# Where a matmul's stream begins in SBUF relative to its weights: 448 instead of 32 bytes, modulo 512

## The chip, the cores and the metric

The kernel runs on one core of a Trainium2 chip. The metric is the device time of one execution in microseconds; a kernel is run several times and the median is taken. PE is the matmul engine (its weight loads are profiled apart, as PEld), DVE, ACT and POOL are the vector, scalar and general engines, and SP issues the transfers.

## What is computed

A decoder trunk of two layers on 256 tokens of width 1024, all in float32. The part that the change is about is the feed-forward block and the projections around it:

```python
for layer in range(DEPTH):
    h = rmsnorm(x, norm_mix[layer])
    z = h @ w_in[layer]
    ...
    x = x + jnp.concatenate([o_a, o_b, o_c, o_d], axis=-1) @ w_out[layer]
    h = rmsnorm(x, norm_ffn[layer])
    x = x + (jax.nn.silu(h @ w_gate[layer]) * (h @ w_up[layer])) @ w_down[layer]
return rmsnorm(x, norm_final)
```

The four head groups (o_a to o_d) are small attention and matrix-memory mixers on 64-wide heads. The hidden width of the feed-forward block is 2816.

## The kernel before, in words

Every weight matrix streams in once, in units of 128 rows by 1024 columns (512 KB). `weight_unit` (line 226) issues the transfer into `wraw`, lets ACT round it to `whi` and DVE form the rest, `wlo`; each of the three tiles has four buffers. Activations are kept in the same two halves, so a product is made of three matmuls: high times high, high times low, low times high.

A matmul has a stationary operand, 128x128, which PE loads first, and a moving operand, which it streams, up to 512 columns of four bytes in each partition. The kernel uses both assignments:

- **The activations are stationary, the weights stream.** `columns` (line 909) for the input projection (tile `zp`, 512 or 404 columns at a time), and `wide` (line 1048) for the second layer's w_down (tiles `dn`, 512 columns, and `dnl`, 256 columns).
- **The weights are stationary, the activations stream.** `wide_T` (line 955) for w_out (tile `op`, the stream is `oT`) and for the first layer's w_down (tile `dn`, the stream is `gT`), and `columns_T` (line 940) for gate and up of both layers (tile `f`, the stream is `hT`).

In the second case `product_T` (line 245) makes the product. Where an accumulator has a whole bank (512 columns), one matmul streams both halves of the activations, 512 columns, against `whi` (line 250), and a second one streams the high half, 256 columns, against `wlo` (line 251). This text calls the two a pair. Where an accumulator has half a bank, `product` (line 240) makes three matmuls of 256 columns (lines 241 to 243). Half banks: all of w_out, the first two of the eleven groups of 512 columns of each layer's gate and up, and two of the eight output blocks of the first layer's w_down. All the rest of gate, up and the first w_down goes in pairs.

`shifted` (line 271) sets where the activations begin inside their tile. If they will be streamed, it skips `SHIFT` elements (line 31), else none:

```python
def shifted(a, n, moving):
    a = a[:, SHIFT if moving else 0:]
    return a[:, 0:n * 2 * SEQ].rearrange("p (k a t) -> p k a t", a=2, k=n)
```

`Norm` uses it for `hT` (line 282; moving for the feed-forward block, not for the input projection), and line 1082 for `gT` (moving in the first layer only). All slices of `hT`, `gT`, `oT` and of the weights that are stationary begin at multiples of 512 bytes from the start of their region, so the distance between a stream's first byte and its weights' first byte, modulo 512, is the same for every matmul of a stage.

PE runs its instructions in the order written; the table `ORDER` interleaves the mixers with the input projection, and the feed-forward block has PE to itself.

Of the kernel before, what the change touches and what calls it, by code (L numbers as in the profile page):

```python
# [10 lines left out]
F32 = mybir.dt.float32  # L11
F32R = mybir.dt.float32r
BF = mybir.dt.bfloat16
AF = mybir.ActivationFunctionType
# [4 lines left out]
P = 128  # L19
# [8 lines left out]
DEPTH = 2  # L28
EPS = 1e-6
WARM = 11  # L30
SHIFT = 8
PAD = 8
MID0 = 2
TAIL = 2
# [70 lines left out]
def trunk(ctx, tc, xt, w_in, w_out, w_gu, w_dn, gains, gfin, cmpw, chan, rowp, ident_d, kf, kb, out):  # L105
    nc = tc.nc
    V, S, G, T = nc.vector, nc.scalar, nc.gpsimd, nc.tensor

    const = ctx.enter_context(tc.tile_pool(name="const", bufs=1))
    par = ctx.enter_context(tc.tile_pool(name="par", bufs=1))  # L110
    wp = ctx.enter_context(tc.tile_pool(name="wp", bufs=2))
    work = ctx.enter_context(tc.tile_pool(name="work", bufs=1))
# [24 lines left out]
    def kc(n, rows=P):  # L137
        return kft[0:rows, KOFF[n]:KOFF[n] + _KC[n]]
# [50 lines left out]
    def bcast(ap):  # L189
        return ap.partition_broadcast(P)  # L190

    def load_positions(l):
        d = {'ch': par.tile([P, 554], F32, name="chan")}
        nc.sync.dma_start(d['ch'][:, 0:32], chan[l, :, 0:32])
        d['posr'] = d['ch'][:, 0:32].rearrange("p (q m c) -> p q m c", q=8, m=2)
        return d

    def load_params(l, d):
        ch = d['ch']
        nc.sync.dma_start(ch[:, 32:], chan[l, :, 32:])  # L200
        d['conv'] = ch[:, 32:42].rearrange("p (b j) -> p b j", b=2)
        d['wqk'] = ch[:, 42:554].rearrange("p (i b n) -> p i b n", i=2, b=2)
        rw = par.tile([P, 456], F32, name="rowp")
        nc.sync.dma_start(rw, bcast(rowp[l]))
        d['gateb'] = rw[:, 0:8]
        d['mnorm'] = rw[:, 8:264]
        d['lamv'] = rw[:, 264:392].rearrange("p (a b) -> p a b", a=4)
        d['dnorm'] = rw[:, 392:456]

        lam_init = 0.8 - 0.6 * math.exp(-0.3 * l)  # L210
        lp = par.tile([P, 2, 32], F32, name="lp")
        ls = par.tile([P, 2], F32, name="ls")
        V.tensor_tensor(out=lp, in0=d['lamv'][:, 0:4:2, :], in1=d['lamv'][:, 1:4:2, :], op=OP.mult)
        V.tensor_reduce(out=ls, in_=lp, op=OP.add, axis=AX.X)
        le = par.tile([P, 2], F32, name="le")
        S.activation(le, ls, AF.Exp)
        d['nlam'] = par.tile([P, 1], F32, name="nlam")
        V.scalar_tensor_tensor(out=d['nlam'], in0=le[:, 1:2], scalar=-lam_init, in1=le[:, 0:1],
                               op0=OP.add, op1=OP.subtract)
        d['subg'] = par.tile([P, HD], F32, name="subg")  # L220
        V.tensor_scalar(d['subg'], d['dnorm'], 1.0 - lam_init, None, op0=OP.mult)
        d['hgh'] = par.tile([P, 256], F32, name="hgh")
        V.tensor_scalar(d['hgh'], d['mnorm'], 0.5, None, op0=OP.mult)
# [47 lines left out]
# [7 lines that stand above are left out]
    class Norm:  # L278
        def __init__(self, g, moving):
            self.g = g  # L280

            hl = shifted(work.tile([P, KB * 2 * SEQ + SHIFT], F32R, name="hT", bufs=1), KB, moving)
            self.x2 = [hl[:, k] for k in range(KB)]
# [79 lines left out]
    def mixer_a(l, z, d):  # L363
# [41 lines left out]
        for c in range(2):  # L405
# [3 lines left out]
                        in1=kc('bdk')[:, :, None].to_broadcast([P, 2, NCMP]), op=OP.mult)  # L409
# [3 lines left out]
                        in1=kc('bd60')[:, :, None].to_broadcast([P, NH, HD]), op=OP.mult)  # L413
# [13 lines left out]
                T.matmul(pcs[:, (t * 2 + b) * 30:(t * 2 + b + 1) * 30], q0[:, b, t * P:(t + 1) * P],  # L427
                         kcb.rearrange("p a n -> p (a n)"), start=True, stop=True)
        yield
        gs = par.tile([P, 2, 12], F32, name="gs")  # L430
        S.activation(gs, z[:, :, COL['ag']:COL['ag'] + 12], AF.Tanh, scale=0.5)
        V.tensor_scalar(gs, gs, 0.5, 0.5, op0=OP.mult, op1=OP.add)

# [418 lines left out]
    d = None  # L852
    for l in range(DEPTH):
# [18 lines left out]
        def group(f):  # L872
            o = work.tile([P, 2, 256], F32, name="o", bufs=2)
            yield from f(l, z, d, o)
            return o

        fs = dict(Z=lambda: mixer_a(l, z, d), A=lambda: mixer_a2(l, z, d), C=lambda: group(mixer_c),
                  B=lambda: group(mixer_b), D=lambda: group(mixer_d))
        gens = {}

        def emit(steps):
            for token in steps.split():
                n = token[0]
                if n == 'w':
                    cur['cmpw'] = [weight_unit(cmpw[l, :, u * 1024:(u + 1) * 1024]) for u in range(2)]
                    continue
                if n == 'p':
                    load_params(l, d)
                    load_consts()
                    continue  # L890
                if n in 'acbd':
                    finish('acbd'.index(n), cur[n.upper()])
                    continue
                if n not in gens:
                    gens[n] = fs[n]()
                for _ in range(int(token[1:] or 1)):
                    try:
                        next(gens[n])
                    except StopIteration as r:
                        cur[n] = r.value  # L900
                        if n == 'A':
                            oT[0] = r.value
# [173 lines left out]
        if l + 1 < DEPTH:  # L1076
            d = load_positions(l + 1)
            load_params(l + 1, d)
        else:
            gf = work.tile([P, D], F32, name="gfin", tag="hT", bufs=1)  # L1080
            nc.sync.dma_start(gf, bcast(gfin[0]))
        gT = shifted(bigp.tile([P, NFB * 2 * SEQ + SHIFT], F32R, name="gT", tag="big"), NFB, l + 1 < DEPTH)

# [227 lines left out]
```

## Time and profile before

| | |
|---|---|
| median of 3 runs | 666.11 us (664.45 to 667.17) |
| the profiled execution | 665.1 us |
| its span, first to last instruction | 663.3 us |
| granted PE clock, share of full speed | 0.994 |
| PE busy | 649.6 us of 3993 matmul records |
| DVE, ACT, POOL busy | 481.4, 384.4, 50.6 us |

The span is what the trace shows; the profiled execution's own time lies 1.8 us above it. A matmul's listed duration holds its passage through the array too, and matmuls overlap, so the step from the start of one to the start of the next is the time that it costs. The timeline gives these starts.

### The profile page before, as it was taken

The numbers are of one execution on the slowest core, as the hardware profiler recorded it, in microseconds if no ns is written. First come the engines' busy times: TensorE is split into PE (matmuls) and PEld (weight loads), VectorE is DVE, ScalarE is ACT, GpSimd is POOL, SyncE is SP. The second block draws the span as 40 slices with busy tenths as digits, with TensorE's granted clock in tenths as the row PEclk, the third lists the DMA queues.
The fourth block names the chain that finished last, engine by engine and source line by source line (L and its number), as shares of the span: only waits on it lengthen the run. The fifth ranks groups of instructions, "written<-read, shape, count | busy, mean of one in ns | idle before, by whom it ended". The sixth has DMA issues, their size and how long they took to land.

```text
span 663.3 us, 10576 instructions
## 1 busy us (share of the span) xinstructions
PE 649.6 (98%) x3993; PEld 566.1 (85%) x3993; DVE 481.4 (73%) x814; ACT 384.4 (58%) x692; POOL 50.6 (8%) x67
## 2 busy tenths in 40 slices
PE   9989999999999999999999999999999999999996
PEld 6877787899988888999988777889998888888885
DVE  6697887768777877744588978875867777875443
ACT  7555776545565656533376487664655656564332
POOL 0000031100200111000010001041000000000002
PEclk9999999999999999999999999999999999999998
DMA  8856305245566666666638441332566666667631
GB/s 269 268 184 201 114 5 171 69 139 173 172 208 188 188 184 197 190 191 190 182 125 275 148 127 33 103 121 83 152 212 171 192 185 195 190 189 221 188 122 63
DMA packets 32882, 109.09 MB, mean 164 GB/s; under 512 B 4032, under 2 KB 5696, under 8 KB 32832
## 3 DMA queue, kind: packets, MB, share of 16 engines
q1 hardware_dynamic: 32544, 107.91, 53.8%
q8 instruction: 31, 0.51, 0.3%
q10 hardware_dynamic: 288, 0.52, 0.2%
q14 instruction: 19, 0.16, 0.1%
HBM read 107.37 MB, written 1.05 MB: 163 GB/s over the span
## 4 chain that ended last, share of the span: by engine, by line
PE 91%; DVE 4%; ACT 2%; issue 1%; POOL 1%; POOLq 0%; ACTq 0%; DVEq 0%
PE f L250 20%; PE f L251 10%; PE zp L242 6%; PE zp L243 6%; PE zp L241 6%; PE dn L250 5%; PE dn L242 3%; PE dn L241 3%; PE dn L243 3%; PE dn L251 2%; PE f L241 2%; PE f L243 2%; PE f L242 2%; PE op L242 2%; PE op L243 2%; PE op L241 2%
## 5 line engine op out<-in xcount | busy, mean ns | idle before, releaser
L237 DVE TENSOR_TENSOR wlo<-wraw,whi 128x1024 fp32r<-128x1024 f32 (+2 forms) x204 | 242.9, 1192 | 111.9 <-ACT whi L236 110.9
L236 ACT ACTIVATE whi<-wraw 128x1024 fp32r<-128x1024 f32 (+2 forms) x204 | 210.8, 1035 | 173.7 <-PE f L250 45.9
L250 PE MATMUL f<-hT,whi 128*128 128x512 f32 x576 | 199.8, 390 | 0.0
L251 PE MATMUL f<-hT,wlo 128*128 128x256 f32 x576 | 162.4, 282 | 0.0
L250 PEld LDWEIGHTS f<-hT,whi 128*128 128x128 f32 x576 | 108.1, 188 | 22.6
L251 PEld LDWEIGHTS f<-hT,wlo 128*128 128x128 f32 x576 | 108.9, 189 | 0.0
L242 PE MATMUL zp<-wlo,hT 128*128 128x512 f32 (+1 forms) x192 | 76.1, 397 | 2.6 <-DVE wlo L237 2.6
L241 PE MATMUL zp<-whi,hT 128*128 128x512 f32 (+1 forms) x192 | 74.4, 398 | 0.9 <-ACT whi L236 0.9
L243 PE MATMUL zp<-whi,hT 128*128 128x512 f32 (+1 forms) x192 | 75.2, 392 | 0.0
L250 PE MATMUL dn<-gT,whi 128*128 128x512 f32 x132 | 46.7, 390 | 0.0
L242 PEld LDWEIGHTS zp<-wlo,hT 128*128 128x128 f32 x192 | 36.4, 190 | 9.5 <-DVE wlo L237 4.7
L241 PEld LDWEIGHTS zp<-whi,hT 128*128 128x128 f32 x192 | 36.4, 191 | 7.4 <-ACT whi L236 2.0
L243 PEld LDWEIGHTS zp<-whi,hT 128*128 128x128 f32 x192 | 36.3, 189 | 5.0
L251 PE MATMUL dn<-gT,wlo 128*128 128x256 f32 x132 | 37.2, 282 | 0.0
L241 PE MATMUL f<-hT,whi 128*128 128x256 f32 x128 | 36.5, 285 | 0.0
L243 PE MATMUL op<-oT,wlo 128*128 128x256 f32 x128 | 36.3, 284 | 0.0
L241 PE MATMUL op<-oT,whi 128*128 128x256 f32 x128 | 36.3, 284 | 0.0
L242 PE MATMUL op<-oT,whi 128*128 128x256 f32 x128 | 35.9, 280 | 0.0
L243 PE MATMUL f<-hT,wlo 128*128 128x256 f32 x128 | 35.7, 279 | 0.0
L242 PE MATMUL f<-hT,whi 128*128 128x256 f32 x128 | 35.7, 279 | 0.0
L250 PEld LDWEIGHTS dn<-gT,whi 128*128 128x128 f32 x132 | 24.8, 188 | 4.4
L242 PE MATMUL dn<-wlo,gT 128*128 128x512 f32 x66 | 26.0, 394 | 0.0
(299 smaller groups left out, 1157.9 us busy)
## 6 DMA issues: line engine op xcount, KB each, us to landing
wraw<-in_w_gu_dram SPq DMA_DIRECT2D x88, 512.0 KB, 3.9
wraw<-in_w_dn_dram SPq DMA_DIRECT2D x44, 512.0 KB, 3.7
wraw<-in_w_in_dram SPq DMA_DIRECT2D x36, 512.0 KB, 4.5
wraw<-in_w_out_dram SPq DMA_DIRECT2D x16, 512.0 KB, 3.5
wraw<-in_w_in_dram SPq DMA_DIRECT2D x8, 404.0 KB, 3.2
wraw<-in_w_in_dram SPq DMA_DIRECT2D x8, 256.0 KB, 4.4
wraw<-in_cmpw_dram SPq DMA_DIRECT2D x4, 512.0 KB, 4.8
xr<-in_xt_dram SPq DMA_DIRECT2D x8, 128.0 KB, 4.2
```

Of the source, the lines that this page charges most:

```text
L236: S.activation(hi[:, c], raw[:, c], AF.Copy)
L237: V.tensor_tensor(out=lo[:, c], in0=raw[:, c], in1=hi[:, c].bitcast(F32), op=OP.subtract)
L241: T.matmul(acc, xh, wh, start=first, stop=False)
L242: T.matmul(acc, xh, wl, start=False, stop=False)
L243: T.matmul(acc, xl, wh, start=False, stop=last)
L250: T.matmul(acc, wh, x2.rearrange("p a t -> p (a t)"), start=first, stop=False)
L251: T.matmul(acc[:, 0:SEQ], wl, xh, start=False, stop=last)
```

## The change

The constant `SHIFT` goes from 8 to 112 elements, 32 to 448 bytes. That makes the tiles of `hT` and `gT` 416 bytes longer in each partition. To make room and to set the places of what lies behind, the small tile `le` is dropped (the exponential is written over its input `ls`) and `gs` (96 bytes) moves from the pool `par`, which lies ahead of the weights, to the pool `work`, which lies behind `hT`.

```diff
@@ -28,7 +28,7 @@
 DEPTH = 2
 EPS = 1e-6
 WARM = 11
-SHIFT = 8
+SHIFT = 112
 PAD = 8
 MID0 = 2
 TAIL = 2
@@ -212,10 +212,9 @@
         ls = par.tile([P, 2], F32, name="ls")
         V.tensor_tensor(out=lp, in0=d['lamv'][:, 0:4:2, :], in1=d['lamv'][:, 1:4:2, :], op=OP.mult)
         V.tensor_reduce(out=ls, in_=lp, op=OP.add, axis=AX.X)
-        le = par.tile([P, 2], F32, name="le")
-        S.activation(le, ls, AF.Exp)
+        S.activation(ls, ls, AF.Exp)
         d['nlam'] = par.tile([P, 1], F32, name="nlam")
-        V.scalar_tensor_tensor(out=d['nlam'], in0=le[:, 1:2], scalar=-lam_init, in1=le[:, 0:1],
+        V.scalar_tensor_tensor(out=d['nlam'], in0=ls[:, 1:2], scalar=-lam_init, in1=ls[:, 0:1],
                                op0=OP.add, op1=OP.subtract)
         d['subg'] = par.tile([P, HD], F32, name="subg")
         V.tensor_scalar(d['subg'], d['dnorm'], 1.0 - lam_init, None, op0=OP.mult)
@@ -427,7 +426,7 @@
                 T.matmul(pcs[:, (t * 2 + b) * 30:(t * 2 + b + 1) * 30], q0[:, b, t * P:(t + 1) * P],
                          kcb.rearrange("p a n -> p (a n)"), start=True, stop=True)
         yield
-        gs = par.tile([P, 2, 12], F32, name="gs")
+        gs = work.tile([P, 2, 12], F32, name="gs")
         S.activation(gs, z[:, :, COL['ag']:COL['ag'] + 12], AF.Tanh, scale=0.5)
         V.tensor_scalar(gs, gs, 0.5, 0.5, op0=OP.mult, op1=OP.add)
```

The built program places the tiles so (first byte in the partition, modulo 512; of a stream, in brackets, how far past its stationary operand it begins, modulo 512):

```
                                      before        after
wraw, whi, wlo                        448           320
hT, tile; read by the projection      448 (0)       320 (0)
hT, feed-forward stream               480 (32)      256 (448)
gT, first layer, stream               480 (32)      256 (448)
gT, second layer, stationary          448 (0)       320 (0)
oT, stream of w_out                   384 (448)     256 (448)
zbig (mixers), stationary with ident  448 (192)     320 (320)
ident, constants, xr                  unchanged
pTa, stream against exts              384 (384)     256 (480)
hg, fth, us, rope2, sq                0             288
```

The order of the instructions is the same on every engine, row by row, with the same waits; only the two rows that wrote and read `le` now name `ls`.

## Rows read from the trace of the kernel before

**Rows 1.** The page: the span, and each engine's busy time with its instructions

```profile
span 663.3 us, 10576 instructions
PE 649.6 (98%) x3993; PEld 566.1 (85%) x3993; DVE 481.4 (73%) x814; ACT 384.4 (58%) x692; POOL 50.6 (8%) x67
```

**Rows 2.** The page: shares of the chain that ended last, by line

```profile
PE f L250 20%; PE f L251 10%; PE zp L242 6%; PE zp L243 6%; PE zp L241 6%; PE dn L250 5%; PE dn L242 3%; PE dn L241 3%; PE dn L243 3%; PE dn L251 2%; PE f L241 2%; PE f L243 2%; PE f L242 2%; PE op L242 2%; PE op L243 2%; PE op L241 2%
```

**Rows 3.** Busy time by stage: stretch and length, then each engine

```profile
core 0: us, PE busy (x) PEld busy (x) DVE busy (x) ACT busy (x) POOL busy (x), PEclk, DMA share, GB/s
...
163.70:272.10 108.40, 108.40 (x650) 97.04 (x649) 84.69 (x113) 63.44 (x94) 16.75 (x11) 1.00 0.63 186
...
272.20:333.20 61.00, 61.00 (x397) 55.81 (x396) 32.43 (x39) 25.81 (x30) 0.00 (x0) 1.00 0.66 194
...
470.40:595.30 124.90, 124.90 (x792) 113.52 (x792) 95.88 (x133) 74.63 (x111) 0.95 (x2) 1.00 0.63 185
...
595.30:648.80 53.50, 53.50 (x287) 45.96 (x286) 26.78 (x28) 21.77 (x23) 0.00 (x0) 1.00 0.56 168
```

**Rows 4.** The page: groups of instructions (busy us, mean ns, idle before)

```profile
L250 PE MATMUL f<-hT,whi 128*128 128x512 f32 x576 | 199.8, 390 | 0.0
...
L251 PE MATMUL f<-hT,wlo 128*128 128x256 f32 x576 | 162.4, 282 | 0.0
...
L250 PE MATMUL dn<-gT,whi 128*128 128x512 f32 x132 | 46.7, 390 | 0.0
...
L251 PE MATMUL dn<-gT,wlo 128*128 128x256 f32 x132 | 37.2, 282 | 0.0
...
L241 PE MATMUL f<-hT,whi 128*128 128x256 f32 x128 | 36.5, 285 | 0.0
```

**Rows 5.** Groups by form, PE, 272.2 to 333.2 us (first layer's w_down)

```profile
L242 PE MATMUL dn<-gT,whi 128*128 128x256 f32 x44 | 12.3, 279 | 0.0
```

**Rows 6.** Timeline, PE, 456.2 to 470.2 us: first and last of 126

```profile
455.92 0.28 PE L242 MATMUL op<-oT,whi 128*128 128x256 f32 x1
...
470.10 0.28 PE L241 MATMUL op<-oT,whi 128*128 128x256 f32 x1
```

**Rows 7.** Timeline, PE, 149.3 to 160.2 us: first and last of 95

```profile
149.12 0.28 PE L242 MATMUL f<-hT,whi 128*128 128x256 f32 x1
...
160.08 0.28 PE L243 MATMUL f<-hT,wlo 128*128 128x256 f32 x1
```

**Rows 8.** Timeline, PE, 200 to 230 us: first and last of 175

```profile
199.67 0.39 PE L250 MATMUL f<-hT,whi 128*128 128x512 f32 x1
...
229.83 0.39 PE L250 MATMUL f<-hT,whi 128*128 128x512 f32 x1
```

**Rows 9.** Groups by form, PE, 595.4 to 648.8 us (second layer's w_down)

```profile
L242 PE MATMUL dn<-wlo,gT 128*128 128x512 f32 x59 | 23.3, 395 | 0.0
...
L243 PE MATMUL dn<-whi,gT 128*128 128x512 f32 x59 | 23.0, 389 | 0.0
...
L243 PE MATMUL dnl<-whi,gT 128*128 128x256 f32 x36 | 10.2, 283 | 0.0
...
L241 PE MATMUL dnl<-whi,gT 128*128 128x256 f32 x36 | 10.1, 280 | 0.0
```

**Rows 10.** Timeline, all engines, 210.05 us on: one stream, one load

```profile
210.07 0.39 PE L250 MATMUL f<-hT,whi 128*128 128x512 f32 x1
...
210.07 0.19 PEld L251 LDWEIGHTS f<-hT,wlo 128*128 128x128 f32 x1
```

**Rows 11.** Lines 292 and 293 (hT is written): ns min, median, max

```profile
L292 ACT ACTIVATE hT<-xr,gain x32: 491/494/511, 4.1 to 474.3; 128x256 fp32r<-128x256 f32 x32
...
L293 DVE SCALAR_TENSOR_TENSOR hT<-xr,gain,hT x32: 474/480/487, 4.6 to 475.0; 128x256 fp32r<-128x256 f32 x32
```

**Rows 12.** Groups, 163.7 to 272.1 us: the split of the weights

```profile
L237 DVE TENSOR_TENSOR wlo<-wraw,whi 128x1024 fp32r<-128x1024 f32 x39 | 47.6, 1222 | 11.6 <-ACT whi L236 11.5
...
L236 ACT ACTIVATE whi<-wraw 128x1024 fp32r<-128x1024 f32 x39 | 41.3, 1059 | 31.2 <-PE f L250 18.5 <-issue 7.0 <-PE f L242 2.9
```


## The prediction

> **What bounds the kernel now.** I read the engines' busy time first, then the chain, the stages, and last the starts of single matmuls. PE is busy for 649.6 of 663.3 us [rows 1], and the chain that ended last is a list of PE lines [rows 2]. The table of stages shows where nothing else counts: in gate and up (163.7 to 272.1 and 470.4 to 595.3 us) and in both w_down stages PE is busy for the whole stretch, at a granted clock of 1.00 or 2.4 GHz [rows 3], and the large groups of matmuls have no idle time before them [rows 4]. Here the end moves only if the step from one matmul's start to the next changes, and there it moves by the full sum.
>
> So the step is what I measure. The kernel already runs one form of matmul, 256 columns streamed against 128x128 weights of the same split, at two distances between stream and weights. In w_out the stream `oT` begins 448 bytes past the weights: 126 matmuls start between 455.92 and 470.10 us, 14.18 us over 125 steps, **113.4 ns** [rows 6]. In the first columns of gate and up `hT` begins 32 bytes past them: 95 matmuls between 149.12 and 160.08 us, 10.96 us over 94 steps, **116.6 ns** [rows 7]. Both stretches are without a gap. The pairs, at distance 32, have 175 matmuls between 199.67 and 229.83 us, 87 pairs in 30.16 us, **346.7 ns** a pair [rows 8]. The change takes all streams at 32 to 448, the distance of w_out.
>
> **The change part by part.**
>
> *The matmuls of 256 columns in threes.* Gate and up have 128 on each of three lines [rows 4], the first w_down 44 on each of three lines, which last 279 ns each [rows 5]; 384 + 132 = 516. If each steps like w_out, 516 x (116.6 - 113.4) = 516 x 3.2 ns = 1.7 us.
>
> *The pairs.* There are 576 + 132 = 708 [rows 4]. Their second matmul has w_out's form. For the first one, 512 columns, no row at 448 exists. I bound it from rows. Listed durations are the step plus a constant (w_out's rows list 0.28 us, the pairs' 0.39 and 0.28), so they can be compared within a shape. The nearest row of 512 columns at another distance is the second w_down, distance 0, where the weights stream: 389 ns on one line and 395 on another, against the pairs' 390 [rows 4, 9]. So the 512-column step can come out 5 ns worse or 1 ns better than now by what was seen. From the other side, if it gains what 256 columns gain, and twice, it gains some 10 ns. The second one's step is about 119 ns by its duration, 282 against the 279 of the threes that step by 116.6; that leaves some 227.7 ns for the first. I take 2 x 113.4 = 226.8 ns for it, w_out's rate per column, since that is 1 ns less, as the 389 ns line is. A pair is then 3 x 113.4 = 340.2 ns, and the gain 708 x (346.7 - 340.2) = 708 x 6.5 ns = 4.6 us.
>
> *What the faster PE leans on.* Each unit needs 1.22 us of DVE and 1.06 us of ACT [rows 12], while PE takes 8 pairs, 2.77 us, over it. DVE is busy for 84.7 of 108.4 us there and ACT for 63.4 [rows 3]; a stretch shorter by 2% takes DVE from 78% to 80%. ACT's idle time ahead of the split is mostly put down to PE itself [rows 12], so the split follows PE and costs nothing. If that cover went, PE would show idle time before line 250; the transfers, at 186 GB/s there, would be next.
>
> *The places of all other tiles.* Everything behind `hT` moves by 384 bytes, the weights by -128. The input projection and the second w_down keep their distance of 0 and w_out its 448: nothing. Transposes in the mixers go from 192 to 320; there are about 100 per layer, and by the 3.2 ns that separate rows 6 and 7 they are worth at most 0.7 us either way, in a part where PE also waits. I take zero. DVE's and ACT's own operands go from multiples of 64 bytes to odd multiples of 32, or back. `hT` shows that this is free: it is written 16 times at either kind of place, and its writes last 491 to 511 ns on ACT and 474 to 487 on DVE over all 32 [rows 11].
>
> *`le` and `gs`.* The same instructions with the same waits; ls is read by no one after the exponential. Zero.
>
> **The sum** is 1.7 + 4.6 = 6.3 us, 0.95%. The profiled execution, 665.1 us with a span of 663.3, would become 658.8; the median of the runs shown lies 1.0 us above it, at 666.1, so I forecast **659.8 us**. The bounds of the 512-column step: with no gain on it a pair gains the 5.6 ns of its second matmul, 4.0 us, together 5.7 us and 660.4; with 10 ns it gains 15.6, 11.0 us, together 12.7 us and 653.4.
>
> **A rule against it.** The rows give two steps for one shape at two distances [rows 6, 7]. The Trainium skill, page "SBUF — State Buffer", section "SBUF: two separate sides", says that within the engine side only the port pair shared by VectorE and GpSimd causes contention and that PE never waits on anyone. By it the sum would be 0. What rows 6 and 7 show does not fit it, unless the 3.2 ns have another cause.
>
> **The rivals.**
>
> *The distance is not the cause; the time stays 666.1.* The two stages differ in more: w_out walks eight half banks per unit, gate and up four, and its stream starts at 384 modulo 512, not at 480, which is no multiple of 64. Against the banks speaks the first w_down, which has other accumulators and the same 279 ns [rows 5]. The start alone is not enough: the second w_down streams from 448, a multiple of 64 too, and its 256-column lines last 280 and 283 ns [rows 9]. And the new place, 256, is like w_out's in that respect also, so that most such causes would give the gain too. The rule above belongs here. Chance 0.12.
>
> *Only the threes gain.* A stream of 512 columns outlasts its load of 128, and both start together (both at 210.07 us, [rows 10]), so the pair may settle into another rhythm in which 448 brings nothing. Then 1.7 us: 664.4. Chance 0.10.
>
> *Slower: the 512-column stream collides at 448.* If stream and load hinder each other where they touch the same part of the 512 bytes, a stream that begins 64 bytes behind the load runs into it early if it is the faster one. With 256 columns this is not seen, but 512 columns have their own cost: at distance 0 they last up to 395 ns while 256 columns last 280 to 283 [rows 9]. With 395 and 283 in a pair (now 390 and 282) it is 6 ns worse, 4.2 us, less the 1.7 of the threes: 668.6. It decides against the change from a pair of 346.7 + 1700/708 = 349.1 ns on. Chance 0.08.
>
> **How the numbers follow.** My forecast, 657 to 662.5 us with the bounds of the 512-column step, gets 0.65; a larger gain, towards the bound of 12.7 us, 0.05; the three rivals 0.30. Half a per cent, 3.3 us, is about what a measurement of this kernel can tell from no change; the lines are 662.8 and 669.4 us. Faster takes the forecast and the larger gain, and a little of the case in which only the threes gain and the pair keeps a part: 0.73. Slower by more than half a per cent is the worse part of the slow rival, 0.05; the rest, 0.22, is the same. The range reaches up to the case of the threes alone, 664.8 with the spread of the runs, and down to 656.0, over half the way to the largest gain: it leaves out about 0.2.
>
> **What would show it.** Right: the line-250 rows fall from 390 to about 388 or 389 ns and line 251's from 282 to 276 or 277; the threes of `f` and of the first w_down from 279 to 276; the stretch of gate and up from 108.4 to about 106.4 us and the second layer's likewise; w_out, the projection and the second w_down unchanged. Wrong: pairs at 346.7 ns again, or line 250 at 395; or PE with idle time before the pairs, which would make the split of the weights the bound; or a gain that sits in the mixers instead.

## The result and the profile after

The changed kernel takes 669.24 us (median of 8 runs, 667.94 to 670.66) against 664.47 us for the kernel before in the same comparison (8 runs): a ratio of 1.0055, 95% interval 1.0036 to 1.0074. It is slower by about half a per cent; 659.8 us, faster by 6.3, was forecast. The profiled execution has a span of 667.1 us, 3.8 more than before [rows 1].

The page of the changed kernel (span; busy time; groups of matmuls with busy us, mean ns of one, idle before; all lines behind the dropped one are numbered one lower):

```profile
span 667.1 us, 10576 instructions
...
PE 653.3 (98%) x3993; PEld 564.9 (85%) x3993; DVE 482.6 (72%) x814; ACT 384.8 (58%) x692; POOL 49.8 (7%) x67
...
L249 PE MATMUL f<-hT,whi 128*128 128x512 f32 x576 | 203.6, 397 | 0.0
...
L250 PE MATMUL f<-hT,wlo 128*128 128x256 f32 x576 | 161.9, 281 | 0.0
...
L249 PE MATMUL dn<-gT,whi 128*128 128x512 f32 x132 | 47.6, 397 | 0.0
...
L250 PE MATMUL dn<-gT,wlo 128*128 128x256 f32 x132 | 37.1, 281 | 0.0
```

The span is longer by 3.8 us, and so about is PE's busy time, 653.3 against 649.6. The groups still have no idle time before them: no wait was added. The 512-column matmul of the pairs lists 397 ns instead of 390 [rows 4], the 256-column one 281 instead of 282. First and last of 171 rows of PE's timeline in the same stretch as [rows 8]:

```profile
199.78 0.40 PE L249 MATMUL f<-hT,whi 128*128 128x512 f32 x1
...
229.81 0.40 PE L249 MATMUL f<-hT,whi 128*128 128x512 f32 x1
```

85 pairs in 30.03 us are **353.3 ns** a pair, 6.6 more than the 346.7 before. The threes (three matmuls of 256 columns) went in two ways. The groups by form of gate and up between 150 and 159 us, then those of the first w_down:

```profile
L241 PE MATMUL f<-hT,whi 128*128 128x256 f32 x27 | 7.5, 276 | 0.0
```

```profile
L241 PE MATMUL dn<-gT,whi 128*128 128x256 f32 x43 | 12.1, 281 | 0.0
```

Gate and up list 276 ns, as hoped, but the first w_down lists 281 instead of 279 [rows 5].

From the starts of the first matmul of each stage in both traces the 3.8 us divide so: the pairs of gate and up take 101.75 us per layer instead of 99.84, twice +1.91; the first w_down 62.19 instead of 61.16, +1.03; the threes of gate and up 22.69 instead of 23.29 and 24.57 instead of 25.05, -0.60 and -0.48. These sum to 3.77 us. The input projections, w_out and the second w_down differ by up to half a microsecond either way, and nearly cancel.

### The profile page after: what moved, and what is told of

Read it like the earlier page. It is cut to its first block, busy times and chain, and to the rows that moved or that the text cites. A ratio compares the mean times of both kernels' runs of the same rounds, so it can differ in the third digit from the quotient of the medians.

```text
span 667.1 us, 10576 instructions
## 1 busy us (share of the span) xinstructions
PE 653.3 (98%) x3993; PEld 564.9 (85%) x3993; DVE 482.6 (72%) x814; ACT 384.8 (58%) x692; POOL 49.8 (7%) x67
## 4 chain that ended last, share of the span: by engine, by line
PE 91%; DVE 3%; ACT 2%; DMA 1%; issue 1%; POOL 1%; SPq 0%; POOLq 0%; ACTq 0%; DVEq 0%
PE f L249 20%; PE f L250 10%; PE zp L241 6%; PE zp L242 6%; PE zp L240 6%; PE dn L249 5%; PE dn L241 3%; PE dn L240 3%; PE dn L242 3%; PE dn L250 2%; PE f L240 2%; PE f L242 2%; PE f L241 2%; PE op L242 2%; PE op L241 2%; PE op L240 2%
## 5 line engine op out<-in xcount | busy, mean ns | idle before, releaser
L249 PE MATMUL f<-hT,whi 128*128 128x512 f32 x576 | 203.6, 397 | 0.0
```

What stands on the lines that cost most here:

```text
L249: T.matmul(acc, wh, x2.rearrange("p a t -> p (a t)"), start=first, stop=False)
```

## The experiments

The theory after the result: the step depends on the **distance** between the stream's first byte and that of the weights, and 448 is a worse place for a 512-column stream than 32. The rivals: the moved tiles do it; the stream's own place does it; only odd or even multiples of 32 count.

**The streams back at 32, everything else as after the change.** Tiles keep their sizes and places, the slice's start becomes a number of its own, so that it can be set apart for both layers' `hT` and for `gT`:

```diff
-        a = a[:, SHIFT if moving else 0:]
+        a = a[:, moving:]
...
-                                         lambda: Norm(gain[:, l, 1], True))
+                                         lambda: Norm(gain[:, l, 1], PLACE[l]))
```

`PLACE` is (8, 8) elements, and 8 for `gT`.

> The tiles lie as after the change, byte for byte; only the streams of hT and gT begin 32 bytes into their tiles again, so the distance to the weights is 32. If the distance (or the place of the stream itself) is the cause: pairs back at 346.7 ns (line 250's matmul 390 ns, line 251's 282), the threes of f at 279 ns, and the time of the kernel before, 664.5 us, within 1.5. If the moved tiles are the cause: pairs stay at 353.3 ns (397 and 281) and the time at 669.

It took 664.95 us (10 runs) against 665.69 (13 runs) for the kernel before, ratio 0.9993, interval 0.9972 to 1.0014. Groups by form of its first gate and up (lines two higher):

```profile
L251 PE MATMUL f<-hT,whi 128*128 128x512 f32 x180 | 62.4, 390 | 0.0
...
L252 PE MATMUL f<-hT,wlo 128*128 128x256 f32 x179 | 50.5, 282 | 0.0
```

Both durations are those of the kernel before, and the two times can't be told apart. So moved tiles, `le` and `gs` cost nothing beyond what this comparison resolves, some 0.3%, and the start of the slice accounts for the change. Weights and streams lie 128 bytes lower here than before, modulo 512, at the same distance.

**Streams, weights and the rest moved together.** From the changed kernel, one tile of 256 bytes leaves `par`. All that lies behind it moves down by 256, but not `gT`:

```diff
-        d['subg'] = par.tile([P, HD], F32, name="subg")
+        d['subg'] = sm.tile([P, HD], F32, name="subg", bufs=1)
```

> As after the change, but a 256-byte tile leaves the part ahead of the weights, so weights, hT and oT all move down by 256 bytes: the feed-forward stream begins at 0 instead of 256 modulo 512, its distance to the weights stays 448. gT does not move, so its distance to the weights becomes 192. If the distance decides: gate and up step as after the change (pairs 353.3 ns, 512-column matmul 397 ns, threes 113.4), and the first w_down does something else. If the stream's own place decides: gate and up change, the first w_down stays at 353.3.

Its groups by form, gate and up first, then the first w_down at distance 192:

```profile
L249 PE MATMUL f<-hT,whi 128*128 128x512 f32 x176 | 62.2, 397 | 0.0
```

```profile
L249 PE MATMUL dn<-gT,whi 128*128 128x512 f32 x116 | 41.9, 398 | 0.0
...
L241 PE MATMUL dn<-gT,whi 128*128 128x256 f32 x38 | 10.7, 281 | 0.0
```

Gate and up stay at 397 ns with the stream at 0 instead of 256. But the first w_down, at 192, lists 398 and 281 ns, where it listed 397 and 281 at 448, so neither expectation is met as a whole. Both results fit a pattern that repeats after 256 bytes and not 512, which the map below bears out. Then weights and streams lie at the same places as in the changed kernel, modulo 256, and this run does not tell the distance from the stream's own place; the next one does. (This kernel and those below were executed once each, but for the one with all streams at 144.)

**Distance 448 to one half of the weights, 32 to the other.** From the kernel before, with a gap between the buffers of `whi` and `wlo` (and without `le`, for room):

```diff
+        wp.tile([P, GAP], F32, name="gap", bufs=1)
         lo = wp.tile([P, 1024], F32R, name="wlo", bufs=4)
```

`GAP` is 104 elements.

> From the kernel before, with 416 bytes between the buffers of whi and those of wlo: the streams of hT and gT then begin 448 bytes past whi and 32 bytes past wlo. While a 512-column matmul (own weights whi) streams, the next weights, wlo, are loaded. If the load in progress is what the stream collides with: 512 columns take 390 ns as at distance 32, a pair about 346.7. If the distance to its own weights counts: 397 ns and about 353.

```profile
L251 PE MATMUL f<-hT,whi 128*128 128x512 f32 x177 | 62.2, 395 | 0.0
...
L252 PE MATMUL f<-hT,wlo 128*128 128x256 f32 x178 | 50.1, 282 | 0.0
```

395 ns is neither 390 nor 397, and by the starts a pair takes 351.1 ns. Neither expectation is met. (The whole, 670.5 us, is longer for other stages too, whose distances the gap changes.) Of what gate and up read, only `whi` has another place modulo 512 than in the first experiment: in the built programs the streams begin at 352 modulo 512 and `wlo` at 320 in both, `whi` at 416 here and at 320 there. The pair goes from 346.7 to 351.1 ns, so the stream's own place does not decide alone; where the weights lie counts. Against the changed kernel, where both distances are 448, the distance to `wlo` is another, and the matmul with `whi` lists 395 ns instead of 397: weights that are not its own may matter to it. The two distances do not simply belong to one matmul each.

**The map.** Five kernels like the first, each with three distances, one for each layer's gate and up and one for the first w_down. At 32 and at 448 these three stretches agree within 0.2 ns a pair, so places tried in different stretches can be compared; the times of the whole kernels, 667.3 to 671.0 us, mix three places and are not. First 0, 64 and 128:

> Tiles as after the change; the streams begin 0 (first layer's gate and up), 64 (second layer's) and 128 bytes (first w_down) past the weights modulo 512. All three starts are multiples of 64. If the distance decides: three different steps of a pair; a stream that starts ahead of the load by more has more room before they meet again, so 64 and 128 should be no worse than 32 (346.7 ns), perhaps near 340, and 0 between 347 and 357 by the second w_down's rows. If only odd against even multiples of 32 count: all three at 353.3 like the change.

Then the rest in steps of 16 bytes, with one place 256 bytes beyond 32:

> Tiles as after the change; distances 96 (first layer's gate and up), 160 (second layer's) and 224 bytes (first w_down). If what counts is the distance modulo 256 (448 and 192 stepped alike: 353.3 ns), and near 32 is the one good place: all three between 347 and 354 ns. If every odd multiple of 32 is like 32: all three near 346.7. If the pair has a better place that no run has met: one of them near 340.

> Distances 16 (first layer's gate and up), 48 (second layer's) and 288 bytes (first w_down). If the pattern repeats after 256 bytes, 288 is the same as 32: 346.7 ns a pair, 390 and 282 ns listed, threes 279. If it repeats after 512 alone, 288 is something else. 16 and 48 lie between 0 (353.3), 32 (346.7) and 64 (348.9): a smooth dependence gives about 350 and 348, a fine-grained one anything.

> Distances 80 (first layer's gate and up), 112 (second layer's) and 144 bytes (first w_down), to fill the map of 16-byte steps. Smooth between 64 (348.9), 128 (350.1) and 192 (353.3): 349 to 351 ns. A place better than 32 would show under 346.

> Distances 176 (first layer's gate and up), 208 (second layer's) and 240 bytes (first w_down), the places shortly behind the load's start when counted modulo 256. Smooth between 192 (353.3) and 0 (353.3): all near 353 and the whole kernel about 4 us slower than before. A fine-grained dependence: at least one of them under 348.

And two kernels between these steps, the second with small distances in other stretches:

> Distances off the 16-byte steps: 8 (first layer's gate and up), 24 (second layer's) and 168 bytes (first w_down), between 0 (353.3), 16 (346.7), 32 (346.7), 160 (346.7) and 176 (350.0). If 346.7 ns, 26.7 above the 768 columns, is the least that a pair costs: none of the three is under 346. If the good place is narrower than 16 bytes and was missed: one of them near 340 ns.

> The same small distances in other stretches: 24 in the first layer's gate and up (353.3 ns in the second layer's), 16 in the second layer's (346.7 in the first's), 8 in the first w_down (353.3 in gate and up). If a pair's step follows from the distance alone: 353.3, 346.7 and 353.3 again. If pairs, like the threes of w_out, can fall into more than one rhythm at one distance: at least one of them differs from the first time by over 1 ns.

The mean time of a pair, from the starts in each stretch, in ns:

```
distance mod 256   0      8      16     24     32     48     64     80     96     112
pair               353.3  353.3  346.7  353.3  346.7  350.0  348.9  353.3  350.0  353.3

distance mod 256   128    144    160    168    176    192    208    224    240
pair               350.3  347.2  346.7  346.7  350.0  353.5  353.3  351.6  349.0
```

Distances 448 (353.3) and 192 (353.5) are the same place here, and 288 gave what 32 gives. The group of the first w_down at 288:

```profile
L251 PE MATMUL dn<-gT,whi 128*128 128x512 f32 x118 | 41.8, 390 | 0.0
...
L252 PE MATMUL dn<-gT,wlo 128*128 128x256 f32 x119 | 33.6, 282 | 0.0
```

It matches [rows 4] to the nanosecond. As far as these two repeats show, the pattern repeats after 256 bytes; it is not smooth, and steps of 16 do not resolve it. The groups by form of 24 bytes between 16 and 32, in the second layer, and again in the other kernel's first layer:

```profile
L251 PE MATMUL f<-hT,whi 128*128 128x512 f32 x256 | 90.5, 397 | 0.0
```

```profile
L251 PE MATMUL f<-hT,whi 128*128 128x512 f32 x176 | 62.2, 397 | 0.0
```

397 ns both times, though 16 and 32 are good places. The pair's time came out within 0.1 ns again when 8, 16 and 24 were tried in another stretch, and 144 within 0.6. Of the rivals, "odd multiples of 32 are good" falls with 96 and 224, "smooth" with 24, and "a better place near 340 ns" with all of them: 346.7 is the least mean that any of the 19 places gave. The kernel before stood at one of the best of them already.

**Half the weights.** From the changed layout, 448 in the first layer's gate and up and 32 elsewhere. Each pair but the first and the last of an accumulation loads 64 columns of weights and streams as before; half of the accumulator's rows are left out:

```diff
-            T.matmul(acc, wh, x2.rearrange("p a t -> p (a t)"), start=first, stop=False)
-            T.matmul(acc[:, 0:SEQ], wl, xh, start=False, stop=last)
+            m = P if first or last else P // 2
+            T.matmul(acc[0:m], wh[:, 0:m], x2.rearrange("p a t -> p (a t)"), start=first, stop=False)
+            T.matmul(acc[0:m, 0:SEQ], wl[:, 0:m], xh, start=False, stop=last)
```

> Leaves out half of the output columns of the pairs in all but the first and the last step of each accumulation: weights of 64 columns are loaded instead of 128, the streams stay as they are. Distance 448 in the first layer's gate and up, 32 in the second layer's and in the first w_down. If a load takes time from the stream that runs beside it: what a pair lasts above 768 columns at 2.4 GHz (320 ns) falls to about half, from 33.3 to some 17 ns at 448 and from 26.7 to some 13 at 32. If the stream of four-byte values has that rate by itself (w_out's 113.4 ns for 256 columns): a pair stays at 340 ns or above at both distances.

Timeline of PE, first and last of 173 rows in the first layer (448), then of 175 in the second (32):

```profile
199.88 0.39 PE L252 MATMUL f<-hT,whi 128*64 128x512 f32 x1
...
229.82 0.39 PE L252 MATMUL f<-hT,whi 128*64 128x512 f32 x1
```

```profile
504.67 0.39 PE L252 MATMUL f<-hT,whi 128*64 128x512 f32 x1
...
534.93 0.39 PE L252 MATMUL f<-hT,whi 128*64 128x512 f32 x1
```

86 pairs in 29.94 us are 348.1 ns, 87 pairs in 30.26 us are 347.8. (A quarter of them, at the ends of each accumulation, still load 128 columns.) So the part above 320 ns does not halve: it stays near 28. (The 320 ns are the expectation's, for 768 columns at one per period of 2.4 GHz; no run here reaches them.) But the two distances no longer differ by the 6.6 ns that they did. At 448 one stretch shows both: by the starts a pair between half loads takes 346.5 ns (207 of them), one between full loads 351.3 (62). At 32 the half load gains nothing: 347.6 ns in the second layer, and in the first w_down 349.3 instead of 346.8. So the shorter load takes away most of what 448 costs, and the 26.7 ns that remain at the best places do not shrink with it. As half of the accumulator's rows are not written either, this run does not show that it is the load and not the writing.

**One place for all.** `hT` and `gT` stream from 144, and where they are stationary they begin 240, 224 and 112 bytes into their tiles. Against a kernel of the map:

```diff
-            nrm = Norm(gain[:, 0, 0], 0)
+            nrm = Norm(gain[:, 0, 0], 60)
...
-            nrm = run(wide_T(w_dn[l], gp, NFB, "dn", lambda: Norm(gain[:, l + 1, 0], 0), True))
+            nrm = run(wide_T(w_dn[l], gp, NFB, "dn", lambda: Norm(gain[:, l + 1, 0], 56), True))
```

> Looks for a kernel that beats both: hT and gT stream from 144 bytes past the weights, where pairs took 347.2 ns and threes 113.8 (32: 346.7 and 116.7). 708 x 0.5 ns lost against 516 x 2.9 ns won is 1.1 us faster than before, under what a measurement tells. Besides, where the weights stream, the activations' start is moved too, so that the weights begin 16 (first input projection), 32 (second) and 144 bytes (second w_down) past them modulo 256 instead of 0: if these places are good in that role as well, 512 columns fall from some 230 to 227 or 228 ns, up to 2 us more. If the map is another one for streams of weights, they stay or rise.

It took 668.01 us against 665.66, ratio 1.0035, interval 1.0012 to 1.0059: slower than before. Groups by form of its second w_down:

```profile
L242 PE MATMUL dn<-whi,gT 128*128 128x512 f32 x54 | 21.4, 397 | 0.0
...
L243 PE MATMUL dn<-wlo,gT 128*128 128x512 f32 x54 | 21.2, 393 | 0.0
...
L244 PE MATMUL dn<-whi,gT 128*128 128x512 f32 x53 | 20.9, 394 | 0.0
```

The same three lines of the changed kernel, where the weights that stream lie at the same places:

```profile
L240 PE MATMUL dn<-whi,gT 128*128 128x512 f32 x55 | 21.6, 393 | 0.0
...
L241 PE MATMUL dn<-wlo,gT 128*128 128x512 f32 x54 | 21.2, 393 | 0.0
...
L242 PE MATMUL dn<-whi,gT 128*128 128x512 f32 x54 | 21.0, 389 | 0.0
```

By the starts (steps of 245 ns and more, which hold a wait, left out) 512 columns take 233.8 ns on average there instead of 229.8, and in the second input projection, at 32, 233.0 instead of 229.4; in the first one, at 16, nothing changes (228.6 both times). So 32, one of the best places for pairs, is a bad one where the weights stream. Only the stationary operand has moved here: again it is not the stream's own place alone. And the threes of gate and up at 144 took 118.7 ns, not the 113.8 that the first w_down had shown at 144.

**What these kernels show of w_out**, which none but the one with the gap changed. Timeline of PE within the first layer's w_out, first and last row: 73 rows of the changed kernel, then 70 of the kernel with distances 96, 160 and 224.

```profile
138.74 0.28 PE L241 MATMUL op<-oT,whi 128*128 128x256 f32 x1
...
146.90 0.28 PE L241 MATMUL op<-oT,whi 128*128 128x256 f32 x1
```

```profile
138.79 0.28 PE L242 MATMUL op<-oT,whi 128*128 128x256 f32 x1
...
146.92 0.28 PE L242 MATMUL op<-oT,whi 128*128 128x256 f32 x1
```

8.16 us over 72 steps are **113.3 ns**; 8.13 us over 69 steps are **117.8 ns**. Up to the first write of `hT` for the feed-forward block, at 146.4 us in the one and 147.5 in the other, the two programs are the same instruction for instruction, with the same tiles at the same places, and w_out's distance is 448 in both. Of 26 stretches of w_out (13 profiled executions with this distance, two layers) 16 ran at 113.3 and 10 at 117.8, none between, and eight of the kernels had one layer at each.

Both stand in the kernel before, too, within one layer. Timeline of PE, first and last of 15 rows of an earlier stretch of its first w_out:

```profile
130.09 0.28 PE L242 MATMUL op<-oT,whi 128*128 128x256 f32 x1
...
131.74 0.28 PE L241 MATMUL op<-oT,whi 128*128 128x256 f32 x1
```

1.65 us over 14 steps are 117.9 ns; from 138.1 us on, behind a stretch of other work, the same layer's w_out steps at 113.3.

## Why the prediction was wrong

**What held.** PE sets the end in these stages, the gain or loss arrives in full: 708 pairs x 6.6 ns = 4.7 us, less 1.0 for the threes in all, and the span moved by 3.8. The split of the weights stayed hidden, moved tiles and `le` and `gs` cost nothing that could be told (ratio 0.9993). The distance does act, by 6.6 ns a pair. The Trainium skill, page "SBUF — State Buffer", section "SBUF: two separate sides", names the port pair shared by VectorE and GpSimd as the only cause of contention on the engines' side, and by that nothing should have changed. That PE waits for no other engine is not contradicted as far as DVE and ACT go: in the changed kernel's first gate and up 286 of 287 pairs take 353 or 354 ns, and the mean is 353.3 both over the 79 in which DVE and ACT are busy all the time and over the 43 in which DVE is idle.

**The step that failed** is the pair, and in it "I take 2 x 113.4 = 226.8 ns for it, w_out's rate per column". By the starts the 512-column matmul takes 235.0 ns where 228.3 were before (227.7 in the prediction's working); the listed 397 ns lies beyond the 395 that bounded it and that the prediction had named as a sign of being wrong. The second half of the step failed too: "Their second matmul has w_out's form" was to bring 113.4 ns, and it stayed at 118.3. A pair went to 353.3 instead of 340.2, so the term of 4.6 us gained is 4.7 us lost.

**Why it failed.** A stage's step was taken for a property of the distance. It is a property of the distance and of the rhythm in which streams and loads follow each other: the same form at 448 takes 113.3 ns in w_out and in gate and up, 117.8 in w_out of another execution, and 117.6 in the first w_down between pairs. What stands in [rows 6] is one of two rhythms, the shorter one; the longer one, 117.9 ns, stood in the same trace, and it is slower than the 116.6 at 32. What it said about 256 columns in unbroken threes held for gate and up (276 ns; 0.6 and 0.5 us gained, where 1.7 were expected for all threes, and 0.1 lost in the first w_down). For a 512-column stream, which runs on after its load, it said nothing, and the only rows on that form at another distance, 389 and 395 ns [rows 9], covered both signs. The weight given to the near end, 389, had no better reason than to the far one.

**Which rival it was.** The slower one: at 448 the 512-column matmul pays. It was priced at 6 ns a pair with a break-even of 349.1; the pair lost 6.6 and went to 353.3. It had listed 395 and 283 ns, and 397 and 281 came. It counted 1.7 us of gain on the threes, and 1.0 came. So it had the right matmul and nearly the right price, at a chance of 0.08. That its 668.6 lies so near to the measured 669.2 is partly luck: it is 2.5 us over the 666.1 it started from, while the spans differ by 3.8 us and the medians of the comparison by 4.8. Its picture, a stream that meets the load when it begins 64 bytes behind it, is supported in part: with half the weights loaded 448 and 32 no longer differ (348.1 and 347.8). That they meet at the start is not shown, and the map, bad at 24 between two good places, is not what that picture gives alone. What collides, and why 26.7 ns above 320 remain at the best places, stays open.

## What to carry to other kernels

A matmul stream of four-byte values can be some 2% faster or slower by where it begins relative to the weights (353.3 against 346.7 ns a pair here), with no idle time to show it; look at the starts and durations of equal matmuls. Do not carry a step from one pattern of matmuls to another, nor from one execution to all: measure the very sequence at the new distance, in more than one stretch. If a slice's start inside a tile of fixed size is the only thing that varies, one kernel can try several places at once, in different layers.

## What was not expected

As far as tried, the dependence repeats after 256 bytes (192 and 448 give 353.5 and 353.3 ns, 32 and 288 both 346.7), and it is finer than 16 (346.7 at 16, 353.3 at 24, 346.7 at 32).

The mean of a stretch can hide a pattern. At 448 and at 32 nearly all pairs are alike, but at 144 three different ones follow each other over and over. Starts of matmuls with `whi` in the first gate and up of the kernel with all streams at 144:

```profile
200.33 0.39 PE L251 MATMUL f<-hT,whi 128*128 128x512 f32 x1
...
200.67 0.40 PE L251 MATMUL f<-hT,whi 128*128 128x512 f32 x1
...
201.03 0.39 PE L251 MATMUL f<-hT,whi 128*128 128x512 f32 x1
...
201.37 0.39 PE L251 MATMUL f<-hT,whi 128*128 128x512 f32 x1
```

To the nanosecond the pairs take 340, 344 and 356 ns in turn. Their mean is 346.7 again, though single pairs do reach 340.

Identical code runs at one of two steady rates, 113.3 or 117.8 ns a matmul in w_out, and keeps it for the whole stretch of some 80 to 100 matmuls looked at; after an interruption by other work it can be the other one. Over the 192 matmuls of a layer's w_out this is up to 0.9 us that no edit explains.
